# Weight sums on GpSimd from two whole chunks, three and a half splits a unit, and the order left to the scheduler, in a Strassen-like feed-forward network

## The chip, the core and the metric

The kernel runs on one core of one Trainium2 chip. A core has a matrix engine (TensorE, "PE" in the profile; its weight loads have a row of their own, "PEld"), VectorE ("DVE"), ScalarE ("ACT"), GpSimd ("POOL") and SyncE ("SP"), which here issues most DMAs. Each engine takes its own instructions in order and waits on semaphores for the others. SBUF is the on-chip memory of 128 partitions; PSUM holds TensorE's results in eight banks of 512 fp32 columns. The metric is device time in microseconds of one execution of the whole program, as a median over runs.

## The reference

Two layers; in each, a SwiGLU network, a token mixer and a second SwiGLU network, each added to the residual x (512 tokens, 1024 features). The change touches the SwiGLU networks alone:

```python
def swiglu(h, w_gate, w_up, w_down):
    return (jax.nn.silu(h @ w_gate) * (h @ w_up)) @ w_down

for l in range(DEPTH):                                   # DEPTH = 2
    x = x + 0.5 * swiglu(rms_norm(x, ffn1_norm[l]), ffn1_w_gate[l], ffn1_w_up[l], ffn1_w_down[l])
    ...                                                  # mixer: convolution and differential attention
    x = x + 0.5 * swiglu(rms_norm(x, ffn2_norm[l]), ffn2_w_gate[l], ffn2_w_up[l], ffn2_w_down[l])
```

The hidden width is 2816, that is 22 blocks of 128.

## The kernel before

Activations lie transposed: features on the partitions, the 512 tokens along the columns. Every fp32 operand is split in two parts of type fp32r: `hi` is the operand rounded to fp32r (ScalarE, L100), `lo` is the operand minus `hi` (VectorE, L101, or GpSimd where so asked). A product is three matmuls: hi x hi, hi x lo, lo x hi.

Each of the four FFNs (two a layer) works through its 22 hidden blocks in three parts, `PARTS`: 5 blocks in the ordinary way, then 8 and 9 with a scheme of seven products in place of eight (Winograd's form of Strassen's). The second and third part have the same shape:

- *Gate and up* (`sums` L135 and `seven` L369, 17 units an FFN, 68 in all). A unit is one hidden block with its gate weights g and up weights u. The input's features are cut in two halves and the tokens in two halves of 256 columns, so that g = (g1, g2), u = (u1, u2), and four combinations of weights are needed besides g1, g2, u2: u2u1 = u2 + u1, g1u2u1, all, and g1u1. `sums` loads a whole chunk of g (1024 columns) and three half chunks, and lets a GpSimd DMA add u1 into two of them (L152); GpSimd then makes the other two sums (L157, L158). Six splits follow: one of 1024 columns (g1 and g2) and five of 512. `seven` runs the products (`go`, L386) in the order u2u1, u2, [rest of the unit before], g1, g2, all, g1u2u1. Each product is 12 matmuls of 256 columns into a half of one of two PSUM banks; ScalarE copies partial results into `keep` (L391, L395, L399), VectorE adds (L400), ScalarE applies SiLU (L401). The seventh product, g1u1, and the three operations that end the block (L405 to L408) are `rest`, which the next unit runs after its second product (`finish`). `Gated.add` then splits the gated block (L549, L550) and, for the first four blocks of a part, forms sums of pairs of blocks (L545 to L562).
- *Down* (`down_sums` L413 and `seven_down` L468, 4 units a part, 32 in all). A unit is two output blocks A and B. The first four hidden blocks go through the seven products (6 matmuls each, L482), the other four or five through plain matmuls of 512 columns (L491): part A into the unit's second bank, part B into a spare bank. GpSimd makes four sums of weights (L442 to L445) and also adds partial results to x (L501, L510); VectorE adds the rest (L513, L516, L520).

Tiles for weights rotate through a few buffers: `RING` gives 5 for raw chunks (`wraw`), 4 each for their parts (`whi`, `wlo`), and 2 each of half width (`wraw2`, `whi2`, `wlo2`). A load waits until a raw buffer is free, a split until a part's buffer is free.

The order on each engine is made by the framework's scheduler when the program is built. `tc.keep_in_program_order` pins single instructions; here, in the units, the first matmul of every product. SyncE's queue issues the loads in order.

Of the kernel before, what the change touches and what calls it, by code (L numbers as in the profile page):

```python
# [11 lines left out]
F32 = mybir.dt.float32  # L12
# [6 lines left out]
P = 128  # L19
DEPTH = 2  # L20
SEQ = 512
# [24 lines left out]
PLAIN = PARTS[0][1]  # L46

# [20 lines left out]
def trunk(ctx: ExitStack, tc: tile.TileContext, xt, par, lamv, relb, onehot,  # L68
# [65 lines left out]

    def sums(g, u):  # L135

        h = slice(0, 512), slice(512, 1024)
        w = {}

        def give(name, t, n, raw):  # L140
            w[name] = tuple(p[:, h[n]] for p in t)
            parts_of(raw, *w[name])
# [9 lines left out]
        nc.gpsimd.dma_start(  # L152
            two.rearrange("p (b c) -> p b c", b=2), u[:, h[0]].unsqueeze(1).broadcast_to([P, 2, 512]), accum_op=ALU.add
        )

        more = ring("wraw")
        G.tensor_tensor(more[:, h[0]], two[:, h[1]], whole[:, h[0]], op=ALU.add)  # L157
        G.tensor_tensor(more[:, h[1]], more[:, h[0]], whole[:, h[1]], op=ALU.add)  # L158
        t = ring("whi"), ring("wlo")
        parts_of(whole, *t)  # L160
        for n, name in enumerate(("g1", "g2")):
            w[name] = tuple(p[:, h[n]] for p in t)
        t = ring("whi"), ring("wlo")
        give("u2u1", t, 0, two[:, h[1]])
        give("g1u2u1", t, 1, more[:, h[0]])
        give("u2", (ring("whi2", 512), ring("wlo2", 512)), 0, u2)
        t = ring("whi"), ring("wlo")
        give("all", t, 0, more[:, h[1]])
        give("g1u1", t, 1, two[:, h[0]])
        return w  # L170
# [198 lines left out]
    def seven(halves, w, banks, fp, before):  # L369

        a, d = banks[0][:, :HS], banks[0][:, HS:]
        b, c = banks[1][:, :HS], banks[1][:, HS:]
        two = banks[1].rearrange("p (n c) -> p n c", n=2)
        keep = fp.tile([P, 4, HS], F32, tag="gn", name="keep", bufs=2)
        g = keep[:, 0::2]

        def go(ps, wt, xt, first=False):


            at = halves.get(xt)
            for j in range(KT // 2):
                (wh, wl), (xh, xl) = wpart(w[wt], j), at(j)
                for i, (l, r) in enumerate(((wh, xh), (wh, xl), (wl, xh))):
                    mm = T.matmul(ps, l, r, start=first and i == j == 0, stop=False, skip_group_check=True)  # L386
                    if i == j == 0:
                        tc.keep_in_program_order(mm)

        go(c, "u2u1", "t1", first=True)  # L390
        S.activation(keep[:, 3], c, AF.Copy)  # L391
        go(d, "u2", "t4", first=True)
        before()
        go(a, "g1", "b11")
        S.activation(keep[:, :2], banks[0].rearrange("p (n c) -> p n c", n=2), AF.Copy)  # L395
        go(b, "g2", "b21")
        go(c, "all", "b22")
        go(a, "g1u2u1", "t2")
        S.activation(keep[:, 2], a, AF.Copy)  # L399
        V.tensor_tensor(two, two, g, op=ALU.add)  # L400
        S.activation(g, two, AF.Silu)  # L401

        def rest():
            go(a, "g1u1", "t3")
            V.tensor_tensor(d, a, keep[:, 3], op=ALU.add)  # L405
            V.tensor_tensor(a, a, keep[:, 1], op=ALU.add)
            us = banks[0].rearrange("p (n c) -> p n c", n=2)
            V.scalar_tensor_tensor(us, us, -1.0, g, op0=ALU.mult, op1=ALU.mult)  # L408
            return banks[0]

        return rest

    def down_sums(dn, m0, many, pairs, q):  # L413

        def pull(raw, at, m, k, end):
            while k < end:
                half, f = divmod(m0 + k, HALF)
                b, w = m * HALF + f, 1
                while (b + w) % 8 and k + w < end and f + w < HALF:
                    w += 1  # L420
                c = b % 8
                nc.sync.dma_start(raw[:, at : at + w * P], dn[half, b // 8][:, c * P : (c + w) * P])
                at, k = at + w * P, k + w

        A, B = 2 * q, 2 * q + 1
        whole, over, J = min(many, 8), max(many - 8, 0), pairs * P
        u, two, g = ring("wraw"), ring("wraw2", 512), ring("wraw")
        pull(u, 0, B, 0, whole)
        pull(g, 0, A, 0, whole)
        pull(two, J, A, whole, many)  # L430
        pull(two, J + over * P, B, whole, many)
        more = ring("wraw")

        def odd_even(t):
            t = t[:, : 2 * J].rearrange("p (j e c) -> p e j c", e=2, c=P)
            return t[:, 0], t[:, 1]

        def row(t, n):
            return t[:, n * J : (n + 1) * J].rearrange("p (j c) -> p j c", c=P)
# [683 lines left out]
```

## Time and profile before

| | us |
|---|---|
| median of 3 runs | 1799.3 |
| lowest, highest of them | 1799.25, 1803.62 |
| the profiled execution | 1802.17 |
| its span, first to last instruction | 1800.2 |

Times are microseconds unless marked ns. In the profile's list of groups, a row is a source line, an engine and an operation, with the tiles written and read, then count, busy time and mean ns of one, and behind the second bar the engine's idle time just before them with what ended it. In the list of waits a row has who waited for whom, the total, how often and the longest. In the timeline a row has start, duration, engine, line and operation, and in brackets the idle time in front of it. In the chain that ended last, a row is a start, a duration and the work, in order of time. In a table by stretches, each engine's busy time stands with the number of its instructions, behind it the granted clock, the DMA engines' share and GB/s. Records of matmuls overlap, since they are pipelined. Line numbers are those of the kernel before.

Where the stages lie in the profiled execution, by the matmuls of L386 and L482: the units of the first FFN run from about 91 to 356 us, of the second from 639 to 906, of the third from 989 to 1255, of the fourth from 1534 to the end. The mixers lie between the first and second, and the third and fourth.

### The profile page before, as it was taken

To read this page: it belongs to the slowest core of one execution; us is meant where nothing else is said; L and a number is where in the kernel's file an instruction comes from. 1 tells how busy PE (TensorE), PEld (TensorE's weight loads), DVE (VectorE), ACT (ScalarE), POOL (GpSimd) and SP (SyncE) were. 2 spreads that over 40 slices of the span, in tenths; PEclk is the share of its full clock that TensorE was granted. 3 is DMA by queue.
4 is the path that set the end of the run, shared out by engine and by line. 5 is a ranking of instruction groups with operands and counts; after the bars stand their busy time and mean duration, and the time that the engine had idled before them with its cause. 6 is when DMAs were issued, how large, how long until landed. Compare 5 with 4: busy or idle time off the path is not lost. (4 is left out here: it accounts for less than half of the span.)

```text
span 1800.2 us, 30317 instructions
## 1 busy us (share of the span) xinstructions
PE 1776.3 (99%) x11437; PEld 1609.4 (89%) x11437; DVE 1343.9 (75%) x2021; ACT 977.6 (54%) x1691; POOL 884.8 (49%) x661
## 2 busy tenths in 40 slices
PE   9999999999999999999999999999999999999999
PEld 7899999888788899899888998998877888999998
DVE  7877687768857868687776776878688587786874
ACT  6465465545844456466543654655457454564652
POOL 2244545669952134444612354356699521345443
PEclk9999999999999999999999999999999999999999
DMA  7374565433122365565433645744331223655752
GB/s 245 109 186 123 146 180 148 139 107 94 47 71 82 94 164 130 141 181 151 127 118 98 165 117 156 185 135 154 93 99 43 71 94 88 167 145 146 181 148 71
DMA packets 112307, 231.36 MB, mean 129 GB/s; under 512 B 12215, under 2 KB 33990, under 8 KB 112160
## 3 DMA queue, kind: packets, MB, share of 16 engines
q1 hardware_dynamic: 92064, 191.93, 33.2%
q0 software_dynamic: 19808, 37.33, 12.2%
q8 instruction: 89, 1.46, 0.3%
q14 instruction: 58, 0.48, 0.1%
q10 hardware_dynamic: 288, 0.16, 0.0%
HBM read 227.26 MB, written 3.42 MB: 128 GB/s over the span
## 5 line engine op out<-in xcount | busy, mean ns | idle before, releaser
L100 ACT ACTIVATE whi<-wraw 128x512 fp32r<-128x512 f32 (+3 forms) x660 | 496.0, 777 | 498.1 <-PE ps_pair L386 135.5
L101 DVE TENSOR_TENSOR wlo<-wraw,whi 128x512 fp32r<-128x512 f32 (+2 forms) x617 | 602.7, 1000 | 179.2 <-ACT whi L100 174.2
L386 PE MATMUL ps_pair<-acth,wlo 128*128 128x256 f32 x1088 | 308.3, 283 | 1.9 <-DVE wlo L101 1.9
L386 PE MATMUL ps_pair<-actl,whi 128*128 128x256 f32 x1088 | 307.9, 283 | 0.0
L386 PE MATMUL ps_pair<-acth,whi 128*128 128x256 f32 x1088 | 307.8, 283 | 0.0
L157 POOL TENSOR_TENSOR wraw<-wraw 128x512 f32<-128x512 f32 x68 | 104.7, 1540 | 309.0 <-DMA wraw<-in_gu 205.5
L386 PE MATMUL ps_pair<-th,whi 128*128 128x256 f32 x816 | 231.7, 284 | 4.8 <-ACT keep L395 3.7
L386 PE MATMUL ps_pair<-th,wlo 128*128 128x256 f32 x816 | 230.9, 283 | 0.0
L386 PE MATMUL ps_pair<-tl,whi 128*128 128x256 f32 x816 | 230.9, 283 | 0.0
L152 POOL DMA_DIRECT2D wraw<-in_gu x68 | 82.0, 1206 | 268.2 <-DVE gs L617 111.9
L386 PEld LDWEIGHTS ps_pair<-acth,wlo 128*128 128x128 f32 x1088 | 208.8, 192 | 2.7 <-DVE wlo L101 2.7
L386 PEld LDWEIGHTS ps_pair<-actl,whi 128*128 128x128 f32 x1088 | 208.8, 192 | 0.3
L386 PEld LDWEIGHTS ps_pair<-acth,whi 128*128 128x128 f32 x1088 | 208.8, 192 | 0.3
L177 PE MATMUL ps_pair<-actl,whi 128*128 128x512 f32 x448 | 174.7, 391 | 0.6 <-DVE actl L263 0.6
L174 PE MATMUL ps_pair<-acth,whi 128*128 128x512 f32 x448 | 173.9, 392 | 0.8 <-ACT whi L100 0.7
L178 PE MATMUL ps_pair<-acth,wlo 128*128 128x512 f32 x448 | 174.2, 390 | 0.0
L386 PEld LDWEIGHTS ps_pair<-th,whi 128*128 128x128 f32 x816 | 156.6, 192 | 6.2 <-ACT keep L395 4.7
L386 PEld LDWEIGHTS ps_pair<-tl,whi 128*128 128x128 f32 x816 | 156.6, 192 | 0.0
L386 PEld LDWEIGHTS ps_pair<-th,wlo 128*128 128x128 f32 x816 | 156.6, 192 | 0.0
L101 POOL TENSOR_TENSOR wlo<-wraw,whi 128x1024 fp32r<-128x1024 f32 x44 | 105.5, 2402 | 37.3 <-ACT whi L100 37.3
L861 DVE SCALAR_TENSOR_TENSOR ps_y<-u,par,ps_y 128x512 f32<-128x512 f32 x156 | 117.6, 754 | 3.7
L158 POOL TENSOR_TENSOR wraw<-wraw 128x512 f32<-128x512 f32 x68 | 116.1, 1707 | 5.3
(214 smaller groups left out, 4177.5 us busy)
## 6 DMA issues: line engine op xcount, KB each, us to landing
wraw<-in_gu SPq DMA_DIRECT2D x208, 256.0 KB, 4.1
wraw<-in_gu SPq DMA_DIRECT2D x104, 512.0 KB, 3.7
wraw<-in_gu POOLq DMA_DIRECT2D x68, 512.0 KB, 5.6
wraw<-in_wqkv SPq DMA_DIRECT2D x24, 512.0 KB, 3.7
wraw<-in_wag SPq DMA_DIRECT2D x16, 512.0 KB, 3.6
wraw<-in_wout SPq DMA_DIRECT2D x16, 512.0 KB, 3.6
wraw<-in_dn SPq DMA_DIRECT2D x60, 128.0 KB, 3.3
wraw<-in_dn SPq DMA_DIRECT2D x20, 384.0 KB, 3.7
```

What stands on the lines that cost most here:

```text
L100: S.activation(hi, raw, AF.Copy)
L101: low = (eng or V).tensor_tensor(out=lo, in0=raw, in1=f32(hi), op=ALU.subtract)
L152: nc.gpsimd.dma_start(two.rearrange("p (b c) -> p b c", b=2), u[:, h[0]].unsqueeze(1).broadcast_to([P, 2, 512]), accum_op=ALU.add)
L157: G.tensor_tensor(more[:, h[0]], two[:, h[1]], whole[:, h[0]], op=ALU.add)
L158: G.tensor_tensor(more[:, h[1]], more[:, h[0]], whole[:, h[1]], op=ALU.add)
L174: first = T.matmul(ps, wh, xh, start=start, stop=False)
L177: T.matmul(ps, wh, xl, start=False, stop=False)
L178: T.matmul(ps, wl, xh, start=False, stop=stop)
L386: mm = T.matmul(ps, l, r, start=first and i == j == 0, stop=False, skip_group_check=True)
L861: V.scalar_tensor_tensor(ys[c] if t == PAD and not n else y, us[c][:, t : t + SEQ], pars[l][:, wc + t : wc + t + 1], y, op0=ALU.mult, op1= ...
```

## The change

The units of both kinds become classes, `GateUp` and `Down`, with a common `body` that runs one unit's products and, between them, prepares the next unit's weights and ends the previous ones. All units of an FFN behind the first five blocks are put in one list.

- Gate and up loads two whole chunks, u and g, and nothing else. GpSimd makes all four sums: d = g1 + u1, u1 += u2 in place, m0 = u1 + g1, m1 = m0 + g2. The adding DMA goes.
- Parts are laid out by the time at which their products run: A = the chunk of u (u2u1, u2), B = the chunk of g (g1, g2), C = m0 and m1 (g1u2u1, all), D = d (g1u1), half as wide. So a unit has three splits of 1024 columns and one of 512.
- A unit's splits are written into the body of the unit before it: A after the first product, B after the second, D and C later, each where a buffer has come free.
- `rest` of the previous unit stays behind the second product; the steps that split its block are spread over the body, and the pair sums (`combine`) move to the body of the unit after that (`prev2.extras`).
- Down: the plain part B runs after the second product, the plain part A after the fourth (`early`, `middle`). In the first unit of a part both go to the end of the unit. GpSimd's two additions to x go; VectorE adds or subtracts `keep` on PSUM and then adds the bank to x (`close`, `into`).
- `PIN = False`: of the new operations none is pinned; the first matmul of each product is, as before.

The diff, cut to its core:

```diff
+PIN = False
...
-    def sums(g, u):
-        ...
-        whole = ring("wraw")
-        nc.sync.dma_start(whole, g)
-        two = ring("wraw")
-        nc.sync.dma_start(two[:, h[0]], g[:, h[0]])
-        nc.sync.dma_start(two[:, h[1]], u[:, h[1]])
-        u2 = ring("wraw2", 512)
-        nc.sync.dma_start(u2, u[:, h[1]])
-        nc.gpsimd.dma_start(
-            two.rearrange("p (b c) -> p b c", b=2), u[:, h[0]].unsqueeze(1).broadcast_to([P, 2, 512]), accum_op=ALU.add
-        )
-        more = ring("wraw")
-        G.tensor_tensor(more[:, h[0]], two[:, h[1]], whole[:, h[0]], op=ALU.add)
-        G.tensor_tensor(more[:, h[1]], more[:, h[0]], whole[:, h[1]], op=ALU.add)
...
+        def sums(self, u1, u2, g1, g2, d, m0, m1):
+            G.tensor_tensor(d, g1, u1, op=ALU.add)
+            G.tensor_tensor(u1, u1, u2, op=ALU.add)
+            G.tensor_tensor(m0, u1, g1, op=ALU.add)
+            G.tensor_tensor(m1, m0, g2, op=ALU.add)
+
+        def hi(self, k, pin=PIN):
+            tag, n = self.WIDE[k]
+            hi, lo = ring("whi" + tag, n), ring("wlo" + tag, n)
+            self.parts[k] = hi, lo
+            pinned(S.activation(hi[:, : self.cols[k]], self.raw[k][:, : self.cols[k]], AF.Copy), pin)
+
+        def lo(self, k, pin=PIN):
+            (hi, lo), c = self.parts[k], self.cols[k]
+            pinned(V.tensor_tensor(out=lo[:, :c], in0=self.raw[k][:, :c], in1=f32(hi[:, :c]), op=ALU.subtract), pin)
...
+        def body(self, nxt, prev, prev2):
+            if nxt:
+                nxt.load()
+            self.begin()
+            self.go(self.c, "u2u1", "t1", first=True)
+            pinned(S.activation(self.keep[:, 3], self.c, AF.Copy))
+            if nxt:
+                nxt.hi("A")
+                nxt.lo("A")
+            self.go(self.d, "u2", "t4", first=True)
+            self.early()
+            if nxt and self.early_free:
+                nxt.hi("B")
+            if prev:
+                prev.rest()
+            self.go(self.a, "g1", "b11")
+            pinned(S.activation(self.keep[:, :2], by_two(self.banks[0]), AF.Copy))
+            if prev:
+                prev.finish(0)
+            if nxt and self.early_free:
+                nxt.lo("B")
+            ...
+            self.go(self.b, "g2", "b21")
+            self.middle()
+            if nxt:
+                nxt.hi("C")
+            if prev2:
+                prev2.extras()
+            self.go(self.c, "all", "b22")
+            self.go(self.a, "g1u2u1", "t2")
+            pinned(S.activation(self.keep[:, 2], self.a, AF.Copy))
+            self.close()
+            if nxt:
+                nxt.lo("C")
+                if not self.early_free:
+                    nxt.hi("B")
+                    nxt.lo("B")
...
+    class GateUp(Unit):
+        ...
+        def load(self):
+            u, g = ring("wraw"), ring("wraw")
+            nc.sync.dma_start(u, self.src[1])
+            nc.sync.dma_start(g, self.src[0])
+            d, more = ring("wraw2", 512), ring("wraw")
+            ...
...
-        G.tensor_tensor(by_two(x[:, B, :]), by_two(x[:, B, :]), keep[:, 1::2], op=ALU.subtract)
...
-        G.tensor_tensor(by_two(x[:, A, :]), by_two(x[:, A, :]), keep[:, 0::2], op=ALU.add)
...
+        def close(self):
+            ...
+            pinned(V.tensor_tensor(two, two, keep[:, 0::2], op=ALU.add))
+            self.into(A, two, 0.5)
+            self.after(A)
+            if not self.early_free:
+                self.spare()
+            two = by_two(self.ps)
+            pinned(V.tensor_tensor(two, two, keep[:, 1::2], op=ALU.subtract))
+            self.into(B, two, 0.5)
...
+            for n, unit in enumerate(units):
+                unit.body(units[n + 1] if n + 1 < len(units) else None, units[n - 1] if n else None,
+                          units[n - 2] if n > 1 else None)
+            units[-1].rest()
```

More of the change, by code (lines that the diff above doesn't have):

```diff
@@ L367, in get, with pinned @@
             return lambda j: (acth[:, k0 + j, c : c + HS], actl[:, k0 + j, c : c + HS])
[L369 to L384, printed above, removed]
+    def pinned(ins, pin=PIN):
+        if pin:
+            tc.keep_in_program_order(ins)
+        return ins
@@ L385, in go @@
                 for i, (l, r) in enumerate(((wh, xh), (wh, xl), (wl, xh))):
[L386 to L387 removed]
+                    mm = T.matmul(ps, l, r, start=first and i == n == 0, stop=False, skip_group_check=True)
+                    if i == n == 0:
                         tc.keep_in_program_order(mm)
[L390 to L391 removed]
@@ L392, in seven @@
[L392 to L409, printed above, removed]
```

439 lines of the change are left out of this document (234 added, 205 removed).

## The prediction

> **What bounds the kernel now.** I read the page's first two parts, then who TensorE's weight loads waited for, then the chain that ended last, then ScalarE, VectorE and GpSimd in single stretches.
>
> ```profile
> PE 1776.3 (99%) x11437; PEld 1609.4 (89%) x11437; DVE 1343.9 (75%) x2021; ACT 977.6 (54%) x1691; POOL 884.8 (49%) x661
> PEclk9999999999999999999999999999999999999999
> ```
>
> TensorE is busy all the time, at full clock. That number alone proves little, since matmuls overlap each other: one record of a 256-wide matmul lasts 283 ns. The pace has to be read from the chain:
>
> ```profile
> 1660.75 86.43 PE ps_pair L386 x720
> 1752.22 3.43 PE ps_pair L491 x15
> 1755.64 0.71 PE ps_pair L482 x6
> 1790.56 1.43 PE ps_pair L482 x12
> 1792.00 3.44 PE ps_d L491 x15
> 1795.46 0.70 DVE x L516
> 1796.29 0.69 DVE x L520
> ```
>
> 720 matmuls of 256 columns in 86.43 us are 0.120 us each, 15 of 512 columns in 3.43 us are 0.229 us. A unit of a gate and up projection has 7 products of 12 matmuls: 84 x 0.120 = 10.08 us. A unit of the down projection has 7 products of 6 and two plain parts of 12 or 15: 42 x 0.120 + 24 x 0.229 = 10.5 us, or 11.9 us. Over the nine units of that row nothing waits: the matmul stream is the floor, and no rearrangement of the other engines gets under it.
>
> The Trainium skill (Trainium Kernel Development and Optimization, Best Practices) says to judge the distance to the roofline by the weight loads' busy share, not by that of the matmuls. By it the 89% above would leave TensorE 1800.2 - 1609.4 = 190.8 us; the chain, which runs on without a gap at 0.120 us, does not agree, and in this text the room is what the waits show.
>
> ```profile
> PEld ps_pair L386 <- ACT keep L395: 4.7, 5, 1.4
> PEld ps_pair L491 <- DVE hl L550: 3.1, 4, 0.9
> PEld ps_pair L482 <- ACT keep L496: 3.0, 6, 1.0
> PEld ps_pair L386 <- DVE wlo L101: 2.7, 4, 1.2
> PEld ps_pair L491 <- ACT hh L549: 2.2, 1, 2.2
> PEld ps_pair L386 <- ACT keep L399: 1.3, 1, 1.3
> ```
>
> These are all the named waits (total us, times, longest) of the stages that the change rewrites: 4.7 + 3.1 + 3.0 + 2.7 + 2.2 + 1.3 = 17.0 us. That is the most that the change can win. The prologue and the two mixers keep theirs.
>
> **The change, part by part.** *Matmuls.* The instruction listing of the changed kernel has the same number of matmuls of each shape. TensorE's floor moves by 0.
>
> *Loads and sums of gate and up.* Before, each of the 68 units loads a whole chunk, three half chunks, and lets a GpSimd DMA add into one of them. After, it loads two whole chunks, and GpSimd makes four sums.
>
> ```profile
> wraw<-in_gu SPq DMA_DIRECT2D x208, 256.0 KB, 4.1
> wraw<-in_gu SPq DMA_DIRECT2D x104, 512.0 KB, 3.7
> wraw<-in_gu POOLq DMA_DIRECT2D x68, 512.0 KB, 5.6
> L152 POOL DMA_DIRECT2D wraw<-in_gu x68 | 82.0, 1206 | 268.2 <-DVE gs L617 111.9 <-DMA wraw<-in_gu 69.5 <-DVE wlo L101 48.4
> L157 POOL TENSOR_TENSOR wraw<-wraw 128x512 f32<-128x512 f32 x68 | 104.7, 1540 | 309.0 <-DMA wraw<-in_gu 205.5 <-DVE wlo L101 44.4 <-DVE ps_pair L400 17.8
> L158 POOL TENSOR_TENSOR wraw<-wraw 128x512 f32<-128x512 f32 x68 | 116.1, 1707 | 5.3
> 229.62 0.60 ACT L395 ACTIVATE keep<-ps_pair 128x512 f32<-128x512 f32 x1 [0.50 <-PE ps_pair L386]
> 232.36 0.63 ACT L100 ACTIVATE whi<-wraw 128x512 fp32r<-128x512 f32 x1 [2.15 <-DMA wraw<-in_gu]
> 233.84 0.63 ACT L100 ACTIVATE whi<-wraw 128x512 fp32r<-128x512 f32 x1 [0.85 <-POOL wraw L157]
> 237.97 0.37 ACT L399 ACTIVATE keep<-ps_pair 128x256 f32<-128x256 f32 x1
> ```
>
> The old chain is load 4.1, adding DMA 5.6, two sums 1.54 + 1.71: 13 us before a split can start. The last four rows show what its lateness costs: ScalarE takes its queue in order, a split stands still for 2.15 us on the DMA and another for 0.85 us on the sum, and the copies of partial sums (`keep`) behind them come late; TensorE then waits for such a copy. The new chain is load 3.7 and one or two sums before chunks D and A can be split: 3.7 + 2 x 1.6 = 6.9 us, 6 us shorter. GpSimd per unit goes from 1.21 + 1.54 + 1.71 = 4.5 us to 4 x 1.6 = 6.5 us of 10.08. It stays hidden while it is under the 10.08, with 3.6 us to spare; beyond that it would pace the units.
>
> *Splits.* Six a unit (one of 1024 columns, five of 512) become three and a half.
>
> ```profile
> L100 ACT ACTIVATE whi<-wraw 128x1024 fp32r<-128x1024 f32 x243 | 255.9, 1057 | 255.0 <-PE ps_pair L177 86.8 <-PE ps_pair L491 41.6 <-PE ps_d L177 39.5
> L100 ACT ACTIVATE whi<-wraw 128x512 fp32r<-128x512 f32 x394 | 232.9, 625 | 218.7 <-PE ps_pair L386 110.3 <-PE ps_d L177 27.5 <-PE ps_pair L482 25.1
> L101 DVE TENSOR_TENSOR wlo<-wraw,whi 128x512 fp32r<-128x512 f32 x394 | 319.5, 836 | 86.9 <-ACT whi L100 86.1
> L101 DVE TENSOR_TENSOR wlo<-wraw,whi 128x1024 fp32r<-128x1024 f32 x199 | 275.0, 1386 | 80.6 <-ACT whi L100 76.4 <-DMA wraw<-in_gu 0.3
> ```
>
> ScalarE: 1.057 + 5 x 0.625 = 4.18 us becomes 3 x 1.057 + 0.625 = 3.80 us. VectorE: 1.386 + 5 x 0.836 = 5.57 us becomes 3 x 1.386 + 0.836 = 4.99 us. Both lie beside TensorE's 10.08 us and are worth nothing by themselves.
>
> *Contention.* Subtractions and sums of weights both read two tensors from SBUF, and they get in each other's way:
>
> ```profile
> 133.10 1.29 POOL L157 TENSOR_TENSOR wraw<-wraw 128x512 f32<-128x512 f32 x1 [4.63 <-DMA wraw<-in_gu]
> 133.26 1.68 DVE L101 TENSOR_TENSOR wlo<-wraw,whi 128x512 fp32r<-128x512 f32 x1 [0.81 <-ACT whi L100]
> 134.47 1.63 POOL L158 TENSOR_TENSOR wraw<-wraw 128x512 f32<-128x512 f32 x1
> 229.15 1.23 DVE L101 TENSOR_TENSOR wlo<-wraw,whi 128x1024 fp32r<-128x1024 f32 x1
> 239.47 0.68 DVE L101 TENSOR_TENSOR wlo<-wraw,whi 128x512 fp32r<-128x512 f32 x1
> 217.00:307.00 90.00, 87.95 (x729) 87.35 (x729) 73.07 (x106) 55.58 (x98) 41.69 (x30) 1.00 0.62 166
> 217.00:307.00 90.00, 46.66 (x52) 0.00 (x0) 1.00 0.62 166
> ```
>
> The subtraction that takes 0.68 us alone took 1.68 us when issued 0.16 us into a sum: it ended 0.55 us after the sum did. The windows (first all engines, VectorE third after the time; then the splits' subtractions alone) give 729 / 84 = 8.7 units, so 73.07 / 8.7 = 8.4 us of VectorE a unit, 46.66 / 8.7 = 5.4 of it subtractions and 3.0 the rest, which stays. After: 3 x 1.23 + 0.68 = 4.4 us alone, + 3.0 = 7.4 us. That leaves 2.7 us, or 0.67 us for each of the four subtractions to wait, before VectorE paces the unit. Bounds of the wait: 0, and one whole sum, 1.29 us (then 7.4 + 5.2 = 12.6 us a unit). GpSimd is at its sums for about half of the unit, and half a sum is 0.65 us, so I take 0.33 us: VectorE 8.7 us, hidden.
>
> The Trainium skill (SBUF — State Buffer, SBUF: two separate sides) has a rule against this change: GpSimd and a VectorE instruction with two SBUF inputs exclude each other for a whole instruction, the later one blocked. The trace agrees: had the two shared the bandwidth, the subtraction would have ended by 133.26 + 2 x 0.68 = 134.62, and it ended at 134.94. By sharing the upper bound of a unit would be 7.4 + 4.4 = 11.8 us, by the rule it is the 12.6 us above; what that would cost is the second rival.
>
> *Down projection.* 32 units. GpSimd loses its two updates of x, VectorE gains two additions on PSUM; sums and loads stay.
>
> ```profile
> L501 POOL TENSOR_TENSOR x<-x,keep 128x512 f32<-128x512 f32 x32 | 52.3, 1633 | 18.9 <-ACT keep L500 18.8
> L510 POOL TENSOR_TENSOR x<-x,keep 128x512 f32<-128x512 f32 x32 | 50.1, 1567 | 18.2 <-ACT keep L509 18.2
> 1791.31 0.38 ACT L509 ACTIVATE keep<-ps_pair 128x256 f32<-128x256 f32 x1 [4.26 <-PE ps_pair L482]
> ```
>
> GpSimd -3.2 us a unit, VectorE + 2 x 0.69 (an operation of that size, as in the chain): hidden, VectorE's unit being 10.5 us or longer. The plain parts move to between the second product and the one after the fourth: more time for the copy at L496. In a part's first unit the plain parts go last, behind the product g1u2u1; the hidden blocks of the last gated unit (L549, L550) get 6 x 0.12 = 0.72 us more. But there only 12 x 0.12 = 1.44 us are left for L496's copy, which stands behind a 1.06 us split and the gate's activation: 0 to 0.5 us at each of 8 places.
>
> *Ends.* At the end of three of the four FFNs (both into a mixer, and the last) the listing has the last two products, g1u2u1 and g1u1, one right behind the other on the same bank. The second must wait for the copy of the first: 0.38 us and two handovers, 0.5 us, three times. Only the last addition to x stands behind TensorE at the kernel's end before; after, a sum and an addition for the other block can stand before it, at most 0.7 us. At the end of the second FFN the scheduler puts the next stage's products between: 0.
>
> *Sum.* Of the 17.0 us I expect the copies L395 and L399 to lose 5.0 of 6.0, the splits 2.0 of 2.7, L549 and L550 3.8 of 5.3 (0.72 us at 5 places), L496 all 3.0, less 8 x 0.25 = 2.0 new: 11.8 won. Lost: 3 x 0.5 + 0.2 = 1.7 at the ends, and 1.6 for the 16 units that complete a pair of blocks and so hold more than the mean on VectorE (0.1 us each, bounds 0 and 0.25). Net -8.5 us. The profiled execution took 1802.2 us (span 1800.2 and 2.0 around it), so 1793.7; the median of the three runs is 2.9 lower, and the same difference gives 1790.8: 1791 us.
>
> **Rivals.** *Waits take the place of waits.* The queues stay in order, so other copies come late, at the ends or in the 8 first down units; half of the gain or none is left. For it: the six rows above name five different causes, and the listing shows wider splits (1.06 for 0.63 us) ahead of the same copies. Against it: load and sums are a unit ahead. Time: 1795 to 1802, say 1798. Within 0.3%. Chance 0.25.
>
> *VectorE becomes the bound of the gate and up units, through the shared SBUF access.* It decides from a mean wait of 0.67 us a subtraction. With GpSimd always at a sum and half a sum in front of each subtraction, 0.65, it just does not; at 0.8 us the unit is 7.4 + 3.2 = 10.6 us, 0.5 over: 68 x 0.5 = 34 us, 1791 + 34 = 1825. At the upper bound 12.6 - 10.08 = 2.5 us x 68 = 170 us: 1961. For it: GpSimd's four sums come in a row. Against: before, with two sums, a subtraction lost only (319.5 + 275.0 - 394 x 0.68 - 199 x 1.23) / 593 = 0.14 us; sums and subtractions laid end to end, 4 x 1.29 + 4.4 = 9.6 us, still fit. Chance 0.12.
>
> *Small losses in a row*: a few tenths at every first down unit, join and pair unit beyond those counted, nothing won elsewhere: 1805 to 1812. Chance 0.11.
>
> That the change does not do what it says is ruled out by the listing (272 sums on GpSimd, no adding DMA); 0.
>
> **Numbers.** Forecast, 1784 to 1794: 0.52. A difference under 0.3%, 5.4 us, can't be told from none: faster means under 1793.9, slower over 1804.7. Faster 0.52, same 0.25, slower 0.23. The range goes down to 1784 (all 17.0 us won) and up to 1812, which takes in the small losses and leaves out the second rival.
>
> **What would show it.** Right: weight loads wait under 6 us in all on the units' lines, no split waits for a DMA in the middle of a part, and every part of nine units runs its 720 matmuls in 86.4 us. The contention step is wrong if VectorE's mean for a subtraction of 1024 columns is over 1.9 us, or its share in the gate and up units over 95%. The ends are wrong if more than 1 us stands between g1u2u1 and g1u1. A gate and up unit longer than 10.2 us makes the forecast wrong.

## The result and the profile after

The changed kernel took 1789.65 us (median of 4 runs, 1787.99 to 1791.85) beside 1801.46 us of the kernel before on the same chip: a ratio of 0.9935, interval 0.9914 to 0.9956, so 0.65% faster. The prediction said 1791. The profiled execution took 1787.99 us, its span 1786.2, against 1802.17 and 1800.2 before.

The page of the changed kernel, first part, and its view of waits: the only row in which a weight load waits on a unit's line (line 377 holds the units' matmuls now; total us, times, longest).

```profile
PE 1771.4 (99%) x11437; PEld 1608.5 (90%) x11437; DVE 1416.0 (79%) x1949; ACT 960.1 (54%) x1555; POOL 950.4 (53%) x665
PEld ps_pair L377 <- ACT keep L426: 3.8, 3, 1.6
```

The six rows that made up 17.0 us before are gone; one new row of 3.8 us has come. TensorE's share is 99% in both kernels and says nothing of this. The chain that ended last (start, us, what) runs through the parts of all four FFNs in long whole pieces; here those of the first and the last FFN:

```profile
90.65 87.87 PE ps_pair L377 x720
206.46 105.69 PE ps_pair L377 x855
1519.89 87.87 PE ps_pair L377 x720
1635.71 105.69 PE ps_pair L377 x855
```

VectorE and GpSimd pay for it. First the windows (time, then PE, PEld, VectorE, ScalarE, GpSimd), then the groups of the subtractions (line 367) and sums:

```profile
90.60:178.50 87.90, 87.90 (x722) 87.29 (x721) 73.93 (x89) 52.18 (x84) 58.55 (x38) 1.00 0.34 104
212.00:300.00 88.00, 88.00 (x736) 88.00 (x735) 80.48 (x92) 53.80 (x85) 57.85 (x37) 1.00 0.38 111
L367 DVE TENSOR_TENSOR wlo<-wraw,whi 128x1024 fp32r<-128x1024 f32 x268 | 396.1, 1480 | 103.3 <-ACT whi L363 101.9
L367 DVE TENSOR_TENSOR wlo<-wraw,whi 128x512 fp32r<-128x512 f32 x116 | 125.6, 1083 | 18.7 <-ACT whi L363 18.3
L354 POOL TENSOR_TENSOR wraw<-wraw 128x512 f32<-128x512 f32 x68 | 116.8, 1717 | 370.6 <-DMA wraw<-in_gu 279.4 <-issue 35.7 <-DVE wlo L367 21.6
L357 POOL TENSOR_TENSOR wraw<-wraw 128x512 f32<-128x512 f32 x68 | 125.5, 1845 | 5.3
```

The first stretch holds 722 / 84 = 8.6 units: VectorE is busy 73.93 / 8.6 = 8.6 us a unit, GpSimd 6.8. It takes in the first units of an FFN, in which VectorE has less to do; the second stretch gives 80.48 / (736 / 84) = 9.2 us. The fairest figure is that of the middle units alone, six from each of the eight parts, 48 in all (sum of those stretches and their mean):

```profile
sum 483.84, PE 483.84 PEld 483.84 DVE 455.07 ACT 304.41 POOL 338.76; mean PE 60.48 PEld 60.48 DVE 56.88 ACT 38.05 POOL 42.34
```

There VectorE is busy 455.07 / 48 = 9.5 us of a unit's 10.08, or 94%. Each subtraction is longer than alone: (268 x (1.480 - 1.23) + 116 x (1.083 - 0.68)) / 384 = 0.30 us of waiting on the mean of all units, those of down among them.

Where the time went, by stages. I cut both traces at the first and the last 256-column matmul of each FFN's units (us):

| stage | before | after | difference |
|---|---|---|---|
| up to the first unit | 90.77 | 90.49 | -0.28 |
| units of FFN 1 | 265.93 | 262.74 | -3.19 |
| mixer 1, plain stage of FFN 2 | 281.99 | 280.51 | -1.48 |
| units of FFN 2, plain stage of FFN 3 | 350.39 | 343.84 | -6.55 |
| units of FFN 3 | 266.01 | 262.74 | -3.27 |
| mixer 2, plain stage of FFN 4 | 279.37 | 279.41 | +0.04 |
| units of FFN 4 | 261.40 | 261.86 | +0.46 |
| behind the last matmul's start | 4.32 | 4.62 | +0.30 |

Sum -13.97, the difference of the spans. The units make -12.55 of it (with the plain stage of FFN 3, which the scheduler mixes with the end of FFN 2), and this contains the three new waits: 1.51, 1.51 and 0.63 us between the last two products of FFN 1, 3 and 4. So old waits worth 12.55 + 3.65 = 16.2 us went, and they went where the six rows stood: by FFN those rows held 4.8, 6.7, 4.8 and 0.6 us, and 4.7, 6.55, 4.8 and 0.2 us went. One of the three places of the new waits, ScalarE first, then TensorE's weight load:

```profile
348.88 1.06 ACT L101 ACTIVATE whi<-wraw 128x1024 fp32r<-128x1024 f32 x1 [1.51 <-PE ps_pair L377]
351.15 1.06 ACT L101 ACTIVATE whi<-wraw 128x1024 fp32r<-128x1024 f32 x1 [1.21 <-PE ps_pair L377]
352.12 0.37 ACT L426 ACTIVATE keep<-ps_pair 128x256 f32<-128x256 f32 x1
352.53 0.30 PEld L377 LDWEIGHTS ps_pair<-hs,whi 128*128 128x128 f32 x2 [1.55 <-ACT keep L426]
```

A split of the mixer's weights stands in front of the copy; it had to wait for a buffer that TensorE gave up late, and the copy waited with it.

Mixer 1's -1.48 us does not come from the change. About 145 us into the mixer the granted clock of the kernel before is 0.50 for 3.41 us, and that of the changed kernel stays at 1.00 (third number from the right; before, then after):

```profile
502.40:505.70 3.30, 3.07 (x10) 2.69 (x11) 3.30 (x12) 3.21 (x11) 1.09 (x1) 0.50 0.00 0
495.00:512.00 17.00, 15.00 (x81) 12.21 (x82) 13.20 (x45) 10.21 (x34) 11.34 (x10) 1.00 0.18 62
```

By the starts of their matmuls the two mixers run level up to this spell and 1.5 us apart behind it. Without it the spans differ by 12.5 us, close to the 11.8 us of the medians.

### The profile page after: what moved, and what is told of

Read it like the earlier page. It is cut to its first block, busy times and chain, and to the rows that moved or that the text cites. A ratio compares the mean times of both kernels' runs of the same rounds, so it can differ in the third digit from the quotient of the medians.

```text
span 1786.2 us, 29641 instructions
## 1 busy us (share of the span) xinstructions
PE 1771.4 (99%) x11437; PEld 1608.5 (90%) x11437; DVE 1416.0 (79%) x1949; ACT 960.1 (54%) x1555; POOL 950.4 (53%) x665
## 4 chain that ended last, share of the span: by engine, by line
PE 96%; DVE 2%; ACT 1%; issue 0%; DMA 0%; SPq 0%; DVEq 0%; ACTq 0%
PE ps_pair L377 53%; PE ps_d L377 6%; PE ps_pair L141 5%; PE ps_pair L142 5%; PE ps_pair L138 5%; PE ps_d L138 2%; PE ps_d L142 2%; PE ps_d L141 2%; PE ps_sc L966 2%; PE ps_pair L842 2%; PE ps_pair L843 2%; PE ps_pair L844 2%; PE ps_out L138 1%; PE ps_out L142 1%; PE ps_out L141 1%; PE ps_v L872 1%
## 5 line engine op out<-in xcount | busy, mean ns | idle before, releaser
L367 DVE TENSOR_TENSOR wlo<-wraw,whi 128x1024 fp32r<-128x1024 f32 (+2 forms) x400 | 534.6, 1342 | 122.0 <-ACT whi L363 120.2
L363 ACT ACTIVATE whi<-wraw 128x1024 fp32r<-128x1024 f32 (+2 forms) x400 | 361.5, 909 | 354.6 <-PE ps_pair L377 188.3
L354 POOL TENSOR_TENSOR wraw<-wraw 128x512 f32<-128x512 f32 (+1 forms) x100 | 145.1, 1451 | 540.9 <-DMA wraw<-in_gu 279.4
L101 ACT ACTIVATE whi<-wraw 128x1024 fp32r<-128x1024 f32 (+3 forms) x124 | 122.6, 999 | 144.4 <-PE ps_pair L141 87.3
L356 POOL TENSOR_TENSOR wraw<-wraw 128x512 f32<-128x512 f32 (+1 forms) x100 | 154.0, 1540 | 7.8
L357 POOL TENSOR_TENSOR wraw<-wraw 128x512 f32<-128x512 f32 (+1 forms) x100 | 153.2, 1532 | 7.8
L355 POOL TENSOR_TENSOR wraw<-wraw 128x512 f32<-128x512 f32 (+1 forms) x100 | 148.1, 1481 | 7.8
```

The costliest lines, as they stand in the source:

```text
L101: S.activation(hi, raw, AF.Copy)
L354: G.tensor_tensor(d, g1, u1, op=ALU.add)
L355: G.tensor_tensor(u1, u1, u2, op=ALU.add)
L356: G.tensor_tensor(m0, u1, g1, op=ALU.add)
L357: G.tensor_tensor(m1, m0, g2, op=ALU.add)
L363: pinned(S.activation(hi[:, : self.cols[k]], self.raw[k][:, : self.cols[k]], AF.Copy), pin)
```

## Experiments

Twelve kernels, each timed in five rounds beside the kernel before, and profiled once. Medians against the changed kernel's 1789.65; ratios are to the kernel before. a_old, a_half, a_sum5 and a_join7 ran on another chip than the rest, on which the kernel before took 1800.7 us (1801.2 and 1802.2 on the first), so the last column is good to some 1.5 us; by the ratios a_join7, for one, is 0.9 us faster than the changed kernel and not 2.6.

| run | median us | ratio to before, interval | against the changed kernel |
|---|---|---|---|
| b_sums | 1853.11 | 1.0298 (1.0272 to 1.0325) | +63.5 |
| a_acc | 1810.28 | 1.0064 (1.0040 to 1.0087) | +20.6 |
| a_old | 1818.31 | 1.0105 (1.0073 to 1.0137) | +28.7 |
| a_half | 1827.04 | 1.0147 (1.0123 to 1.0171) | +37.4 |
| a_sum5 | 1804.53 | 1.0022 (1.0009 to 1.0036) | +14.9 |
| a_late5 | 1800.71 | 0.9995 (0.9982 to 1.0008) | +11.1 |
| a_pin | 1842.66 | 1.0233 (1.0210 to 1.0256) | +53.0 |
| a_gx | 1793.38 | 0.9956 (0.9939 to 0.9972) | +3.7 |
| a_first | 1790.32 | 0.9944 (0.9924 to 0.9965) | +0.7 |
| a_join2 | 1789.21 | 0.9934 (0.9914 to 0.9954) | -0.4 |
| a_join7 | 1787.04 | 0.9930 (0.9911 to 0.9950) | -2.6 |
| a_best1 | 1787.89 | 0.9923 (0.9906 to 0.9940) | -1.8 |

### The sums alone, in the kernel before (b_sums)

```
-        (whole chunk g, halves g1, u2, u2; adding DMA; two sums)
+        two, whole = ring("wraw"), ring("wraw")
+        nc.sync.dma_start(two, u)
+        nc.sync.dma_start(whole, g)
+        d, more = ring("wraw2", 512), ring("wraw")
+        G.tensor_tensor(d, whole[:, h[0]], two[:, h[0]], op=ALU.add)
+        G.tensor_tensor(two[:, h[0]], two[:, h[0]], two[:, h[1]], op=ALU.add)
...
```

> The kernel before, with only the loads and sums of the gate and up projection replaced: two whole chunks and four GpSimd sums in place of four loads, an adding DMA and two sums. Its six splits a unit, its order and its down projection stay. Theory (the lateness of the sums is what made the copies and splits late): the waits on keep (6.0 us before) and on the splits (2.7 us) shrink to under 2 us, time 5 to 9 us under the kernel before, and no split waits over 1 us for a DMA in the middle of a part. Rival (the order in which splits and copies stand in ScalarE's queue made them, and the chain of sums did not): within 2 us of the kernel before, and the waits on keep stay at 4 us or more. Second rival (two more sums a unit on GpSimd slow the subtractions down so far that VectorE is late): slower than before by 5 us or more.

The second rival, by far: 51 us slower than before (2.98%). The sum over this kernel's 48 middle units, then groups and waits (splits are lines 100 and 101 here):

```profile
sum 534.42, PE 497.70 PEld 492.58 DVE 490.91 ACT 312.88 POOL 301.76; mean PE 62.21 PEld 61.57 DVE 61.36 ACT 39.11 POOL 37.72
L101 DVE TENSOR_TENSOR wlo<-wraw,whi 128x512 fp32r<-128x512 f32 x394 | 415.2, 1080 | 64.8 <-ACT whi L100 64.8
PEld ps_pair L379 <- ACT keep L392: 33.5, 18, 2.4
ACT hh L542 <- DVE ps_pair L539: 57.4, 16, 3.6
ACT whi L100 <- DMA wraw<-in_gu: 49.3, 25, 9.1
```

A subtraction of 512 columns takes 1.08 us on the mean (0.836 before), and there are five of them beside the wide one: a unit takes 534.42 / 48 = 11.1 us, 10.2 of it VectorE's, which is more than TensorE's 10.08. ScalarE then waits for VectorE (57.4 us for line 539), its copies come late, and TensorE waits 33.5 us for a copy (and 14.5 us for subtractions themselves). ScalarE's splits also waited 49.3 us for loads, so this run alone does not separate the two causes; a_half does.

### The old chain in the new order (a_acc, a_old)

```
a_acc, second sum:
-            G.tensor_tensor(u1, u1, u2, op=ALU.add)
+            nc.gpsimd.dma_start(u[:, h[0]], self.src[1][:, h[1]], accum_op=ALU.add)
a_old:
+            nc.sync.dma_start(d, self.src[0][:, h[0]])
+            nc.sync.dma_start(u[:, h[0]], self.src[1][:, h[1]])
+            nc.sync.dma_start(u[:, h[1]], self.src[1][:, h[1]])
+            nc.gpsimd.dma_start(u[:, h[0]], self.src[1][:, h[0]], accum_op=ALU.add)
+            nc.gpsimd.dma_start(d, self.src[1][:, h[0]], accum_op=ALU.add)
...
```

> The changed kernel, with one sum of the gate and up units (u1 + u2) again made by an adding DMA that GpSimd issues, between its first and second sum; loads in whole chunks, layout, splits and order stay. Theory (a short chain from load to split is what won): chunk A can be split only after load 3.7, one sum 1.7 and the DMA 5.6, together 11 us, more than a unit's 10.08; 4 to 9 us slower than the changed kernel, with new waits of TensorE on keep or on splits. Rival (layout and order won it): within 2 us of the changed kernel.

> The changed kernel, with the loads and sums of the gate and up units as the kernel before had them (one whole chunk and three halves loaded, u1 added into two places by adding DMAs, here two of 256 KB, and only two sums on GpSimd); layout, splits and order stay. Theory (a late split holds up ScalarE's queue): A and D can be split only after 3.7 + 5.6 = 9.3 us in place of 5.4 to 6.9; the waits on keep come back to 4 us or more, 3 to 12 us slower than the changed kernel. Rival (what cost 20 us in the run with one adding DMA was only that GpSimd itself waited for that DMA between two sums): here no sum waits longer than for a load, within 2 us of the changed kernel, so layout and order alone carry the win.

Theory both times in kind, and more than it said in size: 20.6 and 28.7 us. TensorE's matmuls, ScalarE's copies and splits and VectorE's work stand in the changed kernel's order in a_acc; in a_old the scheduler put all three in another order, so a_acc is the cleaner test. One place in a_acc's timeline, and the windows' row of a stretch that begins there:

```profile
106.09 1.06 ACT L363 ACTIVATE whi<-wraw 128x1024 fp32r<-128x1024 f32 x1 [7.96 <-DMA wraw<-in_gu]
107.06 0.37 ACT L426 ACTIVATE keep<-ps_pair 128x256 f32<-128x256 f32 x1
107.47 0.29 PEld L377 LDWEIGHTS ps_pair<-th,whi 128*128 128x128 f32 x1 [5.31 <-ACT keep L426]
104.80:111.60 6.80, 4.12 (x19) 4.13 (x20) 4.42 (x5) 3.78 (x6) 5.08 (x3) 0.50 0.03 8
```

The split stands 7.96 us for the DMA, the copy right behind it is ready long before, and TensorE loses 5.31 us. The wait is not all: from 104.8 us on the granted clock is 0.50 for 6.83 us. Over the whole span a_acc's waits on keep are 17.7 us more than the changed kernel's and the span is 27.1 us longer; five such spells, 23.9 us in all, can account for the rest, as half of their length is 11.9 us. In a_old, waits and then the timeline of ScalarE and GpSimd:

```profile
PEld ps_pair L377 <- ACT keep L426: 26.4, 22, 2.0
252.68 1.06 ACT L363 ACTIVATE whi<-wraw 128x1024 fp32r<-128x1024 f32 x1 [4.69 <-PE ps_pair L377]
252.73 1.26 POOL L465 TENSOR_TENSOR wraw<-wraw 128x512 f32<-128x512 f32 x1 [6.96 <-issue]
```

The row has grown by 22.6 us of the 26.1 us by which the span is longer; mixer 1, with 6.83 us at a clock of 0.5, makes another 2.4. Split and sum, on two engines, start 0.05 us apart, and both read what the adding DMA writes; the row names TensorE, but that DMA was issued at 244.60 us and landed at 252.61. The rival's time falls, 28.7 us where it said 2. Its mechanism is not excluded: GpSimd does not stand between two sums here, but it stands 6.96 us for the DMA ahead of the first one, and issues the next unit's adding DMAs only behind the second.

### More subtractions (a_half)

The copies to `hi` are cut in the same way as the subtractions shown.

```
+            for a in range(0, c, self.cut):                    # cut = 512 in gate and up units
+                s = slice(a, min(a + self.cut, c))
+                pinned(V.tensor_tensor(out=lo[:, s], in0=self.raw[k][:, s], in1=f32(hi[:, s]), op=ALU.subtract), pin)
```

> The changed kernel, with each split of 1024 columns of the gate and up units made as two of 512, copies and subtractions alike: seven of each a unit in place of four; sums and loads stay. Theory (each subtraction that meets a sum waits for it, so their number sets VectorE's time, and this made the kernel before with only its sums replaced 50 us slower): mean subtraction 1.08 us as there, VectorE 8.6 + 3 x (2 x 1.08 - 1.48) = 10.6 us a unit, over the 10.08; 20 to 45 us slower than the changed kernel. Rival (the order in which the splits stand, not their number, made that): the same sums block no more in total, VectorE stays under 9.5 us a unit, within 5 us of the changed kernel.

Theory: 37.4 us slower. The sum over the 48 middle units, the group and the waits:

```profile
sum 521.20, PE 494.80 PEld 490.75 DVE 497.55 ACT 318.22 POOL 296.96; mean PE 61.85 PEld 61.34 DVE 62.19 ACT 39.78 POOL 37.12
L371 DVE TENSOR_TENSOR wlo<-wraw,whi 128x512 fp32r<-128x512 f32 x524 | 528.6, 1036 | 39.2 <-ACT whi L365 38.5
PEld ps_pair L381 <- ACT keep L430: 34.2, 23, 2.2
```

A unit takes 521.20 / 48 = 10.9 us, 497.55 / 48 = 10.4 of it VectorE's, again more than TensorE's 10.08. The sums are the same, and a subtraction waits about as long as before, 1.036 - 0.68 = 0.36 us on the mean beside 0.30; there are seven of them in a unit in place of four, and this made VectorE the bound.

### One more sum, early and late (a_sum5, a_late5)

```
a_sum5, ahead of the four:
+                G.tensor_tensor(d, g[:, h[0]], u[:, h[0]], op=ALU.add)
a_late5, behind them:
+            G.tensor_tensor(more[:, h[1]], more[:, h[0]], g[:, h[1]], op=ALU.add)
```

> The changed kernel, with one more sum of 512 columns on GpSimd in each gate and up unit (the first one made twice). Theory (GpSimd at 7.0 us a unit and VectorE at 8.6 are hidden behind 10.08, and the mean wait of a subtraction may grow from 0.29 us to 0.67): GpSimd 8.7 us, mean wait about 0.36 us, VectorE 8.9 us: within 2.5 us of the changed kernel. Rival (the shared access of GpSimd and VectorE is already near its bound, as sums and subtractions exclude each other): 8.7 + 4.4 us of GpSimd and VectorE together no longer fit in 10.08, 10 us or more slower.

> The changed kernel, with one more sum of 512 columns on GpSimd in each gate and up unit, as in the run with five sums, but behind the other four (the last one made twice) in place of ahead of them; the order on every engine is else that of the changed kernel. With the sum ahead the time was 15 us longer, and the split of chunk A stood 4.2 us for the second sum. Theory (it was lateness of A, 1.7 us more on its way from the load, in front of the copies in ScalarE's queue): here A is as early as in the changed kernel, only C is later, which has time; within 3 us of the changed kernel, waits on keep under 6 us. Rival (it was the load on the access that GpSimd and VectorE share, which is the same here): 10 us or more slower than the changed kernel.

My theory failed in a_sum5 (+14.9 us, where I had expected 2.5 at most), and the reason I then formed, lateness of chunk A, failed in a_late5: with A as early as in the changed kernel 11.1 of the 14.9 us stayed. Lateness goes with the other 4. It shows in one row of waits, of a_sum5 and then of the changed kernel:

```profile
ACT whi L363 <- POOL wraw L355: 55.4, 28, 4.8
```

```profile
ACT whi L363 <- POOL wraw L355: 2.4, 2, 1.6
```

The rest is the shared access. In the stretch from 212 to 300 us, a_late5's windows and its groups; then the sum over its 48 middle units, and what ScalarE waited for in the whole span:

```profile
212.00:300.00 88.00, 86.11 (x707) 85.34 (x706) 85.86 (x88) 50.96 (x80) 74.32 (x43) 1.00 0.37 108
L367 DVE TENSOR_TENSOR wlo<-wraw,whi 128x1024 fp32r<-128x1024 f32 x27 | 48.6, 1804 | 1.8 <-ACT whi L363 1.8
L367 DVE TENSOR_TENSOR wlo<-wraw,whi 128x512 fp32r<-128x512 f32 x9 | 12.5, 1386 | 0.0
sum 494.85, PE 487.11 PEld 484.59 DVE 480.10 ACT 304.49 POOL 434.98; mean PE 60.89 PEld 60.57 DVE 60.01 ACT 38.06 POOL 54.37
ACT hh L629 <- DVE ps_pair L486: 58.0, 38, 3.5
```

and the changed kernel's groups in the same stretch:

```profile
L367 DVE TENSOR_TENSOR wlo<-wraw,whi 128x1024 fp32r<-128x1024 f32 x27 | 40.3, 1497 | 7.1 <-ACT whi L363 7.0
L367 DVE TENSOR_TENSOR wlo<-wraw,whi 128x512 fp32r<-128x512 f32 x9 | 11.7, 1295 | 0.0
```

Mean wait of a subtraction: (27 x (1.804 - 1.23) + 9 x (1.386 - 0.68)) / 36 = 0.61 us with five sums, (27 x 0.267 + 9 x 0.615) / 36 = 0.35 us with four. This stretch is one of the worse: over all 384 subtractions of the units (means of 1617 and 1137 ns in place of 1480 and 1083) it is 0.41 and 0.30 us. With five, VectorE is busy for 85.86 of 88 us (98%) there and for 97% of the middle units (94% with four); a unit takes 494.85 / 48 = 10.31 us, and ScalarE waits for VectorE. GpSimd itself is idle for 16% of the stretch.

### Order held by hand (a_pin)

```
-PIN = False
+PIN = True
```

> The changed kernel, with the order of copies, splits and subtractions within a unit held as the program gives it, in place of leaving it to the scheduler. Theory (in both orders a copy stands behind at most one split that has its sum, so nothing is late): within 2 us of the changed kernel. Rival (the hand-written order puts splits that still wait for sums or buffers in front of the copies): 5 us or more slower, with waits of TensorE on keep.

The rival's size, 53 us, by another road; waits, then one place in the timeline:

```profile
PEld ps_pair L377 <- DVE hs L647: 38.3, 16, 4.1
262.58 0.42 DVE L647 TENSOR_TENSOR hs<-ps_pair,hs 128x256 fp32r<-128x256 f32 x1
263.05 0.19 PEld L377 LDWEIGHTS ps_pair<-th,whi 128*128 128x128 f32 x1 [3.44 <-DVE hs L647]
```

No split that waits stands in front of a copy here. The combinations of a pair of blocks (lines 640 to 647, 16 times) come late in VectorE's queue; they still read the bank of the unit two before, and it is this bank that the next unit's second product writes.

### Down's updates, the first down unit (a_gx, a_first)

```
a_gx, GpSimd again, behind the copy of keep:
+            G.tensor_tensor(by_two(x[:, m, :]), by_two(x[:, m, :]), self.keep[:, n::2], op=op)
a_first, plain part A of a part's first down unit:
+            self.late()                                   # ahead of g1u2u1, no more behind it
             self.go(self.a, "g1u2u1", "t2")
```

> The changed kernel, with the kept sums of the down projection added to x by GpSimd again (two operations of 1.6 us a unit) in place of two additions of 0.69 us on VectorE in PSUM; all else stays. Theory (both engines have room in these units, and the waits of the down units went with the order of the work ahead of the copies): within 1.5 us of the changed kernel. Rival (GpSimd's updates hold up the next unit's sums behind them, so its splits and the copies behind those): 3 us or more slower, waits on keep return in the down units.

> The changed kernel, with the plain part for block A in the first down unit of each part (8 places) moved to where the kernel before had it, in front of the product g1u2u1, which puts it 0.72 us earlier. Theory (these 0.72 us took away the waits on the hidden blocks hh and hl, 5.3 us before): waits on hh and hl return, 3 to 5 us in all. Rival (the last gated unit now ends early enough by itself, since its splits are no longer late): no waits on them over 1 us in all, and the time within 1.5 us of the changed kernel.

In time a_gx is with the rival, +3.7 us by medians, though its interval overlaps the changed kernel's; its units take 1.9 us more by the profile (stages as above). The waits do not stand where the rival put them: the three new ones, 0.18, 0.52 and 0.86 us, are in gate and up units, and subtractions of 512 columns take 1.15 us for 1.08. In a_first the rival holds: no wait on hh or hl at all, and the units' stages agree within 0.1 us. The 0.72 us were not what removed those waits.

### The joins (a_join2, a_join7, a_best1)

```
a_join2:  self.middle()  (plain part A)    in the last unit, from ahead of "all" to behind g1u2u1
a_join7:  self.early()   (plain part B)    the same
a_best1:  as a_join7 in FFN 1 and 3; FFN 2 untouched; FFN 4: the product "all" behind g1u2u1
```

> The changed kernel, with the plain part for block A in the last unit of each FFN moved between the products g1u2u1 and g1u1 (3.4 us of matmuls on another bank), so that the copy of g1u2u1 has time. Theory (the three waits of 1.51, 1.51 and 0.63 us at these places are that copy, twice behind two splits of the mixer's weights): all three gone, 3.0 to 3.7 us faster than the changed kernel. Rival (the wait moves on: the update of block A, which now starts later, is what the next stage or the end waits for): gain under 1.5 us, and the stretch behind the last matmul grows from 4.6 us by 0.7 us or more.

> The changed kernel, with the plain part for block B (3.4 us of matmuls in a bank of its own) of the last unit of each FFN moved between the products g1u2u1 and g1u1. In the trial that moved block A's plain part the four FFNs' units became 3.9 us shorter, and the second mixer 2.2 us longer, where the scheduler had put 80 matmuls in another order. Theory (the mixer's loss was that order and not a consequence of the join): with 22 matmuls of the mixers in another order here the FFNs gain 3 to 4 us and the mixers lose under 1 us; 2.5 to 4 us faster than the changed kernel. Rival (the late update of a block of x costs the next stage what the join gave): mixers 1 to 3 us longer, gain under 1.5 us.

> The changed kernel, with the joins mended: in the last unit of the two FFNs that a mixer follows, block B's plain part stands between the products g1u2u1 and g1u1; in the last FFN the product all does (0.72 us); the second FFN stays as it is. Theory: waits of 1.51, 1.51 and 0.63 us gone, and the end 0.4 us sooner than in the trial that moved the plain part there too: 2.5 to 4 us faster than the changed kernel, the fastest of all runs. Rival (the stage behind the join gives it back, as its first block of x comes later): under 1.5 us faster.

In all three the waits on keep are gone and the units shrink as expected: FFN 1 and 3 by 1.4 to 1.6 us each, FFN 4 by 0.7. The spans shrink by 1.2, 1.8 and 0.4 us only. What was given back lies elsewhere: mixer 2 +2.2 in a_join2, mixer 1 +1.1 and +1.9 in a_join7 and a_best1, the stage ahead of the first unit +1.0 in a_best1, the end +0.3 to +0.4. Mixer 1's part is not the joins': in a_join7 and a_best1 the granted clock is 0.5 there for 3.41 us, as in the kernel before, and they lose their 1.1 and 1.9 us at that spell; a_half, with the changed kernel's order and joins, has the same spell and took 281.89 us for 280.51. The changed kernel and a_join2 have none there. Mixer 2 of a_join2 has no spell; the scheduler put its matmuls in another order, and whether that or the join costs the 2.2 us stays open. None of the three is faster than the changed kernel beyond the intervals, so my theory of 2.5 us or more is not borne out by the times.

## Why the prediction was right

**The floor and the room.** Right. The matmul stream did not move, and the 17.0 us of named waits were the most there was to win: 16.2 went. The mark for a part (720 matmuls in 86.4 us) was wrong in form: the 720 of the row after contain 12 of 512 columns, 708 x 0.120 + 12 x 0.229 = 87.7 us, and the row says 87.87.

**The chain of loads and sums.** Right, and a_acc shows it best: put the late DMA back, with the order of the other engines untouched, and 21 us are lost, TensorE waiting for copies that stand behind a split in ScalarE's queue; a_old, in another order, loses 29. "It stays hidden while it is under the 10.08, with 3.6 us to spare" was wrong. One more sum of 1.75 us, which leaves GpSimd idle for a sixth of the time, costs 11 us through VectorE. GpSimd's spare time is no room.

**Splits "worth nothing by themselves".** Wrong, and the largest lesson. In VectorE's and ScalarE's busy time the fewer splits save 0.6 and 0.4 us a unit. But with the sums on GpSimd each VectorE instruction that meets a sum waits, and their number decides: seven subtractions for four cost 37 us. The new sums in the old layout and order lose 51 us against the kernel before; the old sums in the new layout and order lose 18 (1818.31 us beside 1800.71); together they win 12. The parts of this change cannot be priced one by one.

**Contention.** The estimate was 0.33 us a subtraction and VectorE 8.7 us a unit. The 0.30 us over all units looks like it, but the estimate itself had a slip: it took GpSimd at its sums for half of a unit, where its own 6.5 us of 10.08 are 64%, which would have given 0.42 us and 9.1 us. In the stretch that is all gate and up it is 0.35 us, and in the middle units VectorE is at 9.5 us, 94% (92 to 96% by part), hardly under the 95% that was named as a sign of being wrong; so "hidden" held with 0.6 us to spare and not 1.4. The point from which the second rival decides, 0.67 us, was too high: at 0.61 us in a_late5's stretch VectorE is at 98% and the unit is already longer. What I left out are VectorE's other instructions on SBUF alone: the subtraction of a held block, 0.42 us before, took 1.52 in all 16 places, once for each block that opens a pair (before, then after):

```profile
L546 DVE TENSOR_TENSOR ps_pair<-hold 128x256 f32<-128x256 f32 x16 | 6.8, 424 | 0.0
L618 DVE TENSOR_TENSOR ps_pair<-hold 128x256 f32<-128x256 f32 x16 | 24.4, 1522 | 0.0
```

The rule of the Trainium skill (SBUF — State Buffer, SBUF: two separate sides), exclusion for a whole instruction, agrees with this row too: 1.1 us is more than the 0.42 us that sharing could add.

**Pair units.** Predicted 1.6 us lost; nothing was, though VectorE holds the 1.1 us more: hidden.

**Down projection.** The 2.0 us of new stalls in the first down units did not come, and hh and hl waited not at all, for another reason than the one given (a_first). "Hidden" holds for the updates as VectorE does them; on GpSimd they cost 1.9 us in the units.

**Ends.** Too low: 1.7 us predicted, 3.65 + 0.30 measured, and with 1.51 us between the last two products the prediction's own sign of wrong ends came true. The handovers were right at the kernel's end (0.63 us). At the two mixers I had not named what else stands in ScalarE's queue: the splits of the next stage's weights.

**The sum.** -8.5 predicted, -14.0 in the profile, -11.8 by medians. Won 16.2 for 11.8 (of which 0.2 is a slip: 0.72 us at 5 places is 3.6, not 3.8), lost 3.95 for 3.3. Of the other 1.7 us in the profile 1.48 are the clock spell in mixer 1 of the kernel before, for which no step stood; the rest came in the stages ahead of the first unit and around mixer 2. That 1791 lies 1.35 us from the median is in part luck: the waits won were put 4.4 us too low, the losses 0.65 us too low, and the 2.9 us from the profiled execution to the median of three runs shrank to 0.7 with the four of the result.

**The rivals.** That waits take the place of waits happened, at the joins only. VectorE as the bound did not happen, but it was nearer than the 0.12 says: one sum more, or three splits cut in two, and it does.

**The order left to the scheduler.** The prediction gave it no price. a_pin shows 53 us.

## What to carry to other kernels

When work moves to an engine that shares an access with another, count how many instructions of that other engine meet it, and not only how long they are: here fewer and wider ones made the move pay. An engine's idle time is no spare room while a neighbour waits for it; find the room by adding one dummy instruction, first early and then late, which separates load from lateness. A copy that frees an accumulator should stand in its queue only behind work whose inputs have arrived, and this holds at stage borders, where the next stage's preparations are queued too.

## What the runs showed of the hardware

VectorE and GpSimd take turns where both read two tensors from SBUF. The changed kernel's timeline of one pair unit, GpSimd's two sums and VectorE's two instructions:

```profile
107.34 1.30 POOL L356 TENSOR_TENSOR wraw<-wraw 128x512 f32<-128x512 f32 x1
108.71 2.15 POOL L357 TENSOR_TENSOR wraw<-wraw 128x512 f32<-128x512 f32 x1
107.56 2.16 DVE L367 TENSOR_TENSOR wlo<-wraw,whi 128x1024 fp32r<-128x1024 f32 x1 [0.38 <-ACT whi L363]
109.64 1.52 DVE L618 TENSOR_TENSOR ps_pair<-hold 128x256 f32<-128x256 f32 x1
```

The subtraction waits until the first sum ends at 108.64; the second sum then waits until the subtraction ends at 109.72; and the short instruction behind it waits for that whole sum, to 110.86, and ends 0.30 us later. When both engines have such work in their queues, a VectorE instruction can wait for a whole sum, short as it may be: all 16 of line 618 took 1519 to 1533 ns. A wide subtraction pays 0.93 us for 1.23 us of work here, the short one 1.1 us for 0.42. This is why the number counts.

The granted clock falls to 0.5 for 3.41 or 6.83 us at a time, and in these traces such spells stand beside waits of TensorE. In a_acc, which has five ahead of its end, each begins within 3 us of the end of a weight load's wait (5.31, 4.8, 2.11 and 2.05 us, and in mixer 1 the last of a row of short ones). Not every wait has one: the changed kernel waits 1.55 us twice and 2.04 us once, and has none ahead of its last 2.6 us. A wait may thus cost more than its length: a_half's span is 38.9 us longer than the changed kernel's, its waits on keep are 30.4 us longer, and half of its five spells of 3.41 us is 8.5. That the waits bring the spells is not shown, since no run holds the clock fixed.

Mixer 1 with the plain stage behind it, which no edit touched, took 280.5 to 283.9 us from kernel to kernel, and the two without a spell there took 280.5 and 280.9. A gain of 1 to 2 us can't be read from the total, only from its own stage and with the clock beside it.
